# A mixture-of-experts stage regrouped: 11 units of three experts in four column groups, instead of 16 pairs in two

## The chip, the core and the metric

The program runs on one core of a Trainium2 chip, as one launch. The metric is device time in microseconds (us). The engines' names in the rows are PE (TensorE, matmul), PEld (TensorE's weight loads), DVE (VectorE), ACT (ScalarE), POOL (GpSimd) and SP (SyncE, which only issues transfers here). "L985" is line 985 of the kernel. GB and MB are decimal.

## What is computed

Two transformer blocks over 256 tokens of width 1024, in float32. The change touches the last part of the first block, a mixture of 32 experts in 4 groups of 8:

```python
def hier_moe(h, w_rg, w_re, w_e_in, w_e_out):
    t = h.reshape(-1, D)                                    # 256 tokens x 1024
    pg = softmax(t @ w_rg); gp, gi = top_k(pg, 1)           # one group of experts for each token
    le = (t @ w_re).reshape(-1, 4, 8)  # ... of the chosen group
    ew, ei = top_k(softmax(le), 2); ew = ew / sum(ew)       # two experts in it
    gates = ...                                             # [32 experts, 256 tokens], two entries for each token
    for wi, wo, ge in zip(w_e_in, w_e_out, gates):          # wi 1024x512, wo 256x1024
        a, u = split(t @ wi, 2)
        acc += ((silu(a) * u) @ wo) * ge[:, None]
```

Before it lie the token mixer of the first block, its output projection (`down` of `w_out`) and the router; behind it the second block, which begins with a norm and a feed-forward part (FFN1, 1024 to 2816 and back). Weights of the experts: 32 x (1024 x 512 + 256 x 1024) x 4 B = 100.66 MB, each read once.

## The kernel before

**Places.** Each expert gets 64 places for tokens (`CAP`). `slot` (L861 and 862) holds for each token and expert the place that the token has, from a running count made by two matmuls. `place(b)` (L827) turns it, for a block of four experts, into a 0/1 matrix `p` of 256 tokens by 256 places: DVE compares `slot` with 1 to 64. `gather` (L945) multiplies the normed tokens, split in a high and a low part (`xrh`, `xrl`, made by `gather_parts`), by that matrix, so that `xg` holds the four experts' tokens side by side, transposed. `way_back` (L959) gives the gate of each place and the transposed matrix. Tokens beyond 64 at one expert go a slow way (`beyond`, behind a branch on `mosti`, the largest load), which every engine tests for itself.

**A unit** is a pair of experts, 16 units. `in_proj` (L977) takes eight steps of k; in a step the two experts' matmuls have 64 columns of weights (`xg`, the tokens) each and 512 columns of data (the expert's w_in), and write the two halves of the partitions of one bank. `act` multiplies silu(a), u and the gate; `turn` transposes; `out_proj` (L1001) takes four steps (two halves n of the 1024 columns, two k), again two matmuls of 64 columns of weights a step; `scatter` (L1011) scales, splits in high and low parts on DVE and ACT, and adds the rows back to the tokens in four accumulators `y`. These matmuls are plain float32, and one of them stands as two instructions in the trace.

**Order.** In the loop over q (L1037), PE runs in_proj(q), way_back(q), scatter(q-1), the gather for the next block, turn(q), out_proj(q), in an order that the scheduler fixes.

**Weights.** All loads of weights are issued by SP, in order. A load waits on SP until the buffer that it fills is free, and everything behind it on SP waits too. A pool `rawp` (5 buffers of 1 MB), `hip` and `lop` (6 each of 0.5 MB) serve the whole kernel: elsewhere `raw` takes a weight panel and `hi` and `lo` its two parts. The experts use `raw` for w_in (`in_load`) and `lop`, `hip`, `gp4` in turn for w_out (`out_load`); ahead of the stage two units and a third unit's w_out are loaded, 14.7 MB, partly in `gp4` (`in_load_ahead`).

Of the kernel before, what the change touches and what calls it, by code (L numbers as in the profile page):

```python
# [9 lines left out]
F32 = mybir.dt.float32  # L10
# [12 lines left out]
CAP = 64  # L23
# [8 lines left out]
def shape_constants():  # L32
# [7 lines left out]
        np.tile(np.eye(64), (2, 2)),  # L40
        np.concatenate([k // 64 == m[:, 0:32], k // 64 == m[:, 0:32] - 2, np.tile(np.arange(1, 65)[None, :], (P, 1))], 1),
# [38 lines left out]
def body(ctx: ExitStack, tc: tile.TileContext, I, out, dbg=None):  # L80
# [14 lines left out]
    psb = ctx.enter_context(tc.tile_pool(name="psb", bufs=4, space=PSUM))  # L95

# [39 lines left out]
    def load(src, a, b):  # L136
        t = rawp.tile([P, 2048], F32, tag="raw", name="raw")
# [105 lines left out]
    V.tensor_copy(CI, v2(cst[:, 4, 0:64]))  # L243
# [174 lines left out]
    tri0 = rawp.tile([P, 2048], F32, tag="raw", name="raw")[:, 0:640]  # L418
    nc.sync.dma_start(tri0, I["cst"][:, 640:])
# [50 lines left out]
    wah = hip.tile([P, 1024], F32R, tag="hi", name="wah")[:, :512].rearrange("p (k f) -> p k f", k=KD)  # L470
# [317 lines left out]
    wi = {}  # L788

    def in_load(q, n):  # L790

        if (q, n) not in wi:
            t = rawp.tile([P, 2, 2, 512], F32, tag="raw", name="raw")
            for i in range(2):
                nc.sync.dma_start(t[:, i], I["w_expert_in"][0, 2 * q + i, 2 * n * P:(2 * n + 2) * P, :]
                                  .rearrange("(k p) f -> p k f", p=P))
            wi[q, n] = [t[:, :, k, :] for k in range(2)]

    def in_load_ahead(q, n, pool, tag):

        ts = [pool.tile([P, D], F32, tag=tag, name="wi").rearrange("p (k f) -> p k f", k=2) for _ in range(2)]
        for i in range(2):
            nc.sync.dma_start(ts[i], I["w_expert_in"][0, 2 * q + i, 2 * n * P:(2 * n + 2) * P, :]
                              .rearrange("(k p) f -> p k f", p=P))
        wi[q, n] = [[t[:, k, :] for t in ts] for k in range(2)]

    def out_load(q, pool, tag):
        halves = []
        for k in range(2):
            for i in range(2):  # L810
                t = pool.tile([P, D], F32, tag=tag, name="wo")
                nc.sync.dma_start(t, I["w_expert_out"][0, 2 * q + i, k * P:(k + 1) * P, :])
                halves.append(t)
        return halves

    for n in range(4):
        in_load(0, n)
    wo = {0: out_load(0, lop, "lo")}
    in_load(1, 0)
    wo[1] = out_load(1, hip, "hi")  # L820
    in_load_ahead(1, 1, hip, "hi")
    in_load_ahead(1, 2, lop, "lo")
    in_load_ahead(1, 3, gp4, "g4")

    places, xgs = {}, {}

    def place(b):  # L827
        p4 = t2("p4", F32R).rearrange("p (t e s) -> p t e s", t=2, e=4)
        for t in ((0, 1) if b == 0 else (slice(0, 2),)):
            n = [P, 4, 64] if b == 0 else [P, 2, 4, 64]  # L830
            V.tensor_tensor(p4[:, t], (iota64[:, None, :] if b == 0 else iota64[:, None, None, :]).to_broadcast(n),
                            slot[:, t, 4 * b:4 * b + 4, None].to_broadcast(n), op=ALU.is_equal)
        places[b] = p4.rearrange("p t e s -> p t (e s)")
        xgs[b] = []


    def tops(src, n, name, then, dt=F32):
# [22 lines left out]
    mm(pc[:, 32:64], onesr, disp[:, 0, :], start=False, stop=True, skip_group_check=True)  # L860
    slot = small(64, "slot", 1).rearrange("p (t f) -> p t f", t=2)  # L861
    placed = V.scalar_tensor_tensor(slot, pc[:, 0:64].rearrange("p (t f) -> p t f", t=2), 1.0, dispf, op0=ALU.add, op1=ALU.mult)
    place(0)

# [5 lines left out]
    gates = cp.tile([P, 2, 32], F32, name="gates")  # L870
# [8 lines left out]
    pc = bank()  # L879
    for t in range(2):  # L880
        mm(pc[:, 0:32], onesr, disp[:, t, :], start=t == 0, stop=t == 1)
    loads = small(32, "loads", 1, I32)
    V.tensor_copy(loads, pc[:, 0:32])
    most = small(1, "most")
    V.tensor_reduce(most, pc[:, 0:32], axis=AX.X, op=ALU.max)
# [88 lines left out]
    def experts(w, i):  # L974
        return w[i] if isinstance(w, list) else w[:, i, :]
# [627 lines left out]
```

## Time and profile before

| | us |
|---|---|
| median of 3 runs (1124.84 to 1125.15) | 1125.04 |
| the profiled execution | 1127.29 |
| its span, first to last instruction | 1125.4 |
| from the first in_proj matmul to the end of the last out_proj | 194.97 to 465.79 |

The span is what the rows show; the execution's own time has 1.89 us around it. The profile's page gives busy times of the engines; a busy PE is one with a matmul in flight. DMA share is the mean busy share of the 16 DMA engines, and it can read a little over 1.

### The profile page before, as it was taken

The numbers are of one execution on the slowest core, as the hardware profiler recorded it, in microseconds if no ns is written. First come the engines' busy times: TensorE is split into PE (matmuls) and PEld (weight loads), VectorE is DVE, ScalarE is ACT, GpSimd is POOL, SyncE is SP. The second block draws the span as 40 slices with busy tenths as digits, with TensorE's granted clock in tenths as the row PEclk, the third lists the DMA queues.
The fourth block names the chain that finished last, engine by engine and source line by source line (L and its number), as shares of the span: only waits on it lengthen the run. The fifth ranks groups of instructions, "written<-read, shape, count | busy, mean of one in ns | idle before, by whom it ended". The sixth has DMA issues, their size and how long they took to land.

```text
span 1125.4 us, 14826 instructions
## 1 busy us (share of the span) xinstructions
PE 1066.3 (95%) x5631; PEld 783.8 (70%) x5632; DVE 666.1 (59%) x1277; ACT 508.3 (45%) x904; POOL 5.6 (0%) x14
## 2 busy tenths in 40 slices
PE   4898998899999998799999999999999999999997
PEld 1585776444444443398888877777888888888886
DVE  3894855233322222596666469878749677666466
ACT  3634544222312211455555446584546455555453
POOL 0000000000000000000000000000000000000000
PEclk8899998999999999899999999999999999999999
DMA  9875976889999999676566634355447555656521
GB/s 377 283 280 204 365 262 260 295 311 342 355 358 380 358 326 369 198 225 199 176 208 206 202 115 156 122 172 156 145 150 261 178 176 177 209 173 220 189 92 38
DMA packets 144769, 260.64 MB, mean 232 GB/s; under 512 B 9404, under 2 KB 76200, under 8 KB 143416
## 3 DMA queue, kind: packets, MB, share of 16 engines
q1 hardware_dynamic: 144464, 259.32, 66.5%
q8 instruction: 45, 0.74, 0.3%
q10 hardware_dynamic: 232, 0.35, 0.1%
q14 instruction: 28, 0.23, 0.1%
HBM read 258.60 MB, written 1.05 MB: 231 GB/s over the span
## 4 chain that ended last, share of the span: by engine, by line
PE 73%; DVE 4%; ACT 2%; issue 1%; DMA 1%; DVEq 0%; ACTq 0%
PE mm L280 19%; PE mm L985 10%; PE mm L282 9%; PE mm L1008 5%; PE acc L302 4%; PE acc L300 4%; PE acc L304 4%; PE mm L943 3%; PE acc L1151 2%; PE acc L1150 2%; PE acc L1158 2%; PE acc L1024 2%; PE acc L1023 1%; PE acc L263 1%; PE acc L264 1%; PE acc L262 1%
## 5 line engine op out<-in xcount | busy, mean ns | idle before, releaser
L166 DVE TENSOR_TENSOR lo<-raw,hi 128x1024 fp32r<-128x1024 f32 (+1 forms) x240 | 287.2, 1205 | 161.0 <-ACT hi L165 157.1
L165 ACT CAST hi<-raw 128x1024 fp32r<-128x1024 f32 (+1 forms) x240 | 246.7, 1036 | 219.8 <-PE mm L280 94.7
L280 PE MATMUL mm<-xT,hi 128*128 128x512 f32 x832 | 209.7, 394 | 0.6 <-DVE rs L1430 0.6
L280 PEld LDWEIGHTS mm<-xT,hi 128*128 128x128 f32 x832 | 149.5, 189 | 27.5 <-DVE rs L1430 1.0
L985 PE MATMUL mm<-raw,xg 128*64 128x512 f32 x488 | 122.0, 598 | 0.0
L282 PEld LDWEIGHTS mm<-xT,lo 128*128 128x128 f32 x832 | 113.6, 190 | 8.1
L282 PE MATMUL mm<-xT,lo 128*128 128x256 f32 x832 | 116.3, 283 | 0.0
L985 PEld LDWEIGHTS mm<-raw,xg 128*64 128x64 f32 x488 | 35.1, 137 | 65.0 <-issue 61.2
L1008 PE MATMUL mm<-wo,z 128*64 128x512 f32 x256 | 58.8, 601 | 1.0 <-DVE z L999 1.0
L262 PE MATMUL acc<-hi,xT 128*128 128x512 f32 x144 | 57.7, 402 | 0.0
L263 PE MATMUL acc<-hi,xT 128*128 128x512 f32 x144 | 57.4, 398 | 0.0
L264 PE MATMUL acc<-lo,xT 128*128 128x512 f32 x144 | 57.1, 399 | 0.0
L990 ACT ACTIVATE esg<-mm 128x256 f32<-128x256 f32 x16 | 6.1, 384 | 112.6 <-PE mm L985 112.6
L956 ACT ACTIVATE xg<-mm,shT,gmT 128x256 f32<-128x256 f32 x64 | 32.3, 562 | 53.9 <-PE mm L943 52.5
L302 PE MATMUL acc<-hi,hl 128*128 128x512 f32 x176 | 55.5, 389 | 0.0
L300 PE MATMUL acc<-hi,hh 128*128 128x512 f32 x176 | 55.5, 390 | 0.0
L304 PE MATMUL acc<-lo,hh 128*128 128x512 f32 x176 | 55.5, 389 | 0.0
L1017 DVE TENSOR_TENSOR og<-mm,gtm 128x512 f32<-128x512 f32 x32 | 22.0, 688 | 40.7 <-PE mm L1008 40.7
L943 PE MATMUL mm<-p,xT 128*128 128x256 f32 x256 | 40.2, 306 | 2.1 <-DVEq L897 1.5
L991 DVE SCALAR_TENSOR_TENSOR esg<-esg,gs,mm 128x256 f32<-128x256 f32 x16 | 7.7, 480 | 57.6 <-ACT esg L990 57.6
L165 ACT CAST oh<-og 128x512 fp32r<-128x512 f32 x32 | 19.6, 618 | 47.2 <-DVE og L1017 47.1
L943 PEld LDWEIGHTS mm<-p,xT 128*128 128x128 f32 x256 | 36.4, 208 | 5.0 <-issue 3.3
(458 smaller groups left out, 1612.5 us busy)
## 6 DMA issues: line engine op xcount, KB each, us to landing
raw<-in_w_expert_in_dram SPq DMA_DIRECT2D x122, 512.0 KB
raw<-in_w_in_dram SPq DMA_DIRECT2D x32, 1024.0 KB
wo<-in_w_expert_out_dram SPq DMA_DIRECT2D x64, 512.0 KB
raw<-in_w_ada_dram SPq DMA_DIRECT2D x24, 1024.0 KB
raw<-in_ffn_w_gate_dram SPq DMA_DIRECT2D x22, 1024.0 KB
raw<-in_ffn_w_up_dram SPq DMA_DIRECT2D x22, 1024.0 KB
raw<-in_ffn_w_down_dram SPq DMA_DIRECT2D x22, 1024.0 KB
raw<-in_w_out_dram SPq DMA_DIRECT2D x8, 1024.0 KB
```

The costliest lines, as they stand in the source:

```text
L165: S.copy(hi, src)
L166: return V.tensor_tensor(lo, src, hi.bitcast(F32), op=ALU.subtract)
L262: mm(o, h_[k][:, c], hi[:, kk, z], start=k == starts, stop=False)
L263: mm(o, l_[k][:, c], hi[:, kk, z], start=False, stop=False)
L280: mm(pb, hi[:, k, :], x2[k], start=k == 0, stop=False, skip_group_check=True)
L282: mm(pb[:, 0:256], lo[:, k, :], x2[k][:, 0:256], start=False, stop=k == nk - 1, skip_group_check=True)
L300: mm(pa[t][n], hh[k][:, c], hi[:, 0, n * 512:(n + 1) * 512], start=k == seq[0], stop=False)
L302: mm(pa[t][n], hl[k][:, c], hi[:, 0, n * 512:(n + 1) * 512], start=False, stop=False)
L304: mm(pa[t][n], hh[k][:, c], lo[:, 0, n * 512:(n + 1) * 512], start=False, stop=k == seq[-1])
L943: mm(pb[:, kk * 256:(kk + 1) * 256], (xrh, xrl)[i][:, t, k * P:(k + 1) * P], places[b][:, t, :], start=i == 0 and t == 0 and kk == 0, stop ...
L985: mm(st_["hp"][64 * i:64 * i + 64, :], xgs[q // 2][k // 4][:, k % 4, 64 * e:64 * e + 64], experts(wi[q, k // 2][k % 2], i), start=k == 0, ...
L1008: mm(oo[n][r, :], st_["z"][:, k, r], wo[q][2 * k + i][:, c], start=k == 0, stop=k == 1, skip_group_check=True)
```

## The change

The 32 experts form 11 units of three (the last of two). A unit has four column groups of 32 places: group 0 is shared, groups 1 to 3 belong to the three experts. Whichever expert of the unit has more than 32 tokens (the first such) also owns the shared group, as its places 33 to 64. In the last unit, groups 0 and 1 belong to its first expert, groups 2 and 3 to its second.

```diff
-CAP = 64
+NU = 11
+CAP = 32
...
-    rawp = ctx.enter_context(tc.tile_pool(name="rawp", bufs=5))
-    hip = ctx.enter_context(tc.tile_pool(name="hip", bufs=6))
-    lop = ctx.enter_context(tc.tile_pool(name="lop", bufs=6))
+    def weight_pools(**pools):
+        panels.close()
+        wp_.clear()
+        for name, bufs in pools.items():
+            wp_[name] = panels.enter_context(tc.tile_pool(name=name, bufs=bufs, reuse_waits="tile"))
+    weight_pools(rawp=5, hip=6, lop=6)
...
+    weight_pools(mwp=14)
+    def unit_load(src, e):
+        t = wp_["mwp"].tile([P, 3, 512], F32, tag="mw", name="mw")
+        nc.sync.dma_start(t[:, :len(e)], src.rearrange("e p f -> p e f"))
+        return t
+    def unit_loads(u):
+        e = experts[u]
+        a, b = e[0], e[-1] + 1
+        if u < NU and (u, 0) not in wi:
+            for k in range(KD):
+                wi[u, k] = unit_load(I["w_expert_in"][0, a:b, k * P:(k + 1) * P, :], e)
+            for n in range(2):
+                for k in range(2):
+                    wo[u, k, n] = unit_load(I["w_expert_out"][0, a:b, k * P:(k + 1) * P, n * 512:(n + 1) * 512], e)
+    for u in range(2):
+        unit_loads(u)
...
-    slot = small(64, "slot", 1).rearrange("p (t f) -> p t f", t=2)
+    slot = small(66, "slot", 1).rearrange("p (t f) -> p t f", t=2)
...
+    V.tensor_copy(many[:, 0:32], pc[:, 64:96])
+    V.tensor_scalar(own, many.rearrange("p (u i) -> p u i", i=3), CAP + 0.5, None, op0=ALU.is_gt)
...
+    V.tensor_reduce(slot4[:, :, 0:NU - 1, 0], owned[:, :, 0:NU - 1], axis=AX.X, op=ALU.add)
...
     place(0)
...
-        with tc.If(over > CAP):
+        with tc.If(over > 0):
...
+    def tiles_of(q, w):
+        if q == NU - 1:
+            return [w[:, 0], w[:, 0], w[:, 1], w[:, 1]]
+        i = nc.s_assert_within((owner >> (2 * q)) & 3, 0, 2, skip_runtime_bounds_check_because=
+                               "at most one of a unit's two bits is set: its second or its third expert is the owner")
+        return [w[:, bass.ds(i, 1)]] + [w[:, i] for i in range(3)]
...
-            for i in range(2):
-                e = (2 * q + i) % 4
-                mm(st_["hp"][64 * i:64 * i + 64, :], xgs[q // 2][k // 4][:, k % 4, 64 * e:64 * e + 64],
-                   experts(wi[q, k // 2][k % 2], i), start=k == 0, stop=k == KD - 1, skip_group_check=True)
+            for i, w in enumerate(tiles_of(q, wi[q, k])):
+                c = 128 * (q % 2) + 32 * i
+                mm(st_["hp"][32 * i:32 * i + 32, :], xgs[q // 2][k // 4][:, k % 4, c:c + 32], w,
+                   start=k == 0, stop=k == KD - 1, skip_group_check=True)
...
+    owner = nc.values_load(owners[0:1, 0:1], engines=[mybir.EngineType.PE], min_val=0, max_val=4 ** 11 - 1)
...
-    scattered = scatter(prev, NQ - 1)
+    scattered = scatter(prev, NU - 1)
+    weight_pools(rawp=5, hip=6, lop=6)
```

out_proj changes as in_proj does: four matmuls of 32 columns a step. While the stage runs, the memory of the three pools is one ring `mwp` of 14 tiles; a tile holds one k (or one k and half n of w_out) of all experts of a unit, 3 x 128 x 512 floats or 0.786 MB (0.524 MB in the last unit), so a unit takes 12 tiles, 8 for in_proj and 4 for out_proj, and there are 132. A new tile waits only for the tiles whose memory it takes. The owners of all units are packed in one integer that PE reads into a register, from which the address of the shared group's weights is worked out. The diff also does the same regrouping for the gates (`gate4`, `gsplit`), and small things that follow: a smaller table of constants, `vrow` in another pool, single buffers in `tops`.

On SP, at the start of the stage, before (the places `raw`, `wo`, `wi` are buffers for expert weights, `mosti` the number on which the branch to the slow way hangs):

```order
L795 DMA raw<-in_w_expert_in_dram 128x2x512 x8
L812 DMA wo<-in_w_expert_out_dram 128x1024 x3
L795 DMA raw<-in_w_expert_in_dram 128x2x512 x2
L812 DMA wo<-in_w_expert_out_dram 128x1024 x5
L803 DMA wi<-in_w_expert_in_dram 128x2x512 x6
L812 DMA wo<-in_w_expert_out_dram 128x1024 x4
L896 TENSOR_LOAD mosti
L896 ISA x2
L795 DMA raw<-in_w_expert_in_dram 128x2x512 x10
L897 COMPARE_AND_BRANCH
```

and in the changed kernel (`mw` is a tile of the ring; the eighteen rows of the slow way behind the branch are not shown):

```order
L805 DMA mw<-in_w_expert_in_dram 128x3x512 x8
L805 DMA mw<-in_w_expert_out_dram 128x3x512 x4
L805 DMA mw<-in_w_expert_in_dram 128x3x512 x8
L805 DMA mw<-in_w_expert_out_dram 128x3x512 x4
L942 TENSOR_LOAD mosti
L943 COMPARE_AND_BRANCH
```

The loads of two whole units now stand ahead of SP's branch, 24 tiles for a ring of 14, and 12 each for the units that follow it.

On DVE, between the count of places and the first matrix of places, before (`teo` marks a token's two experts, `xT` is the low part of the tokens):

```order
L850 TENSOR_SCALAR teo<-tew 128x64
L862 SCALAR_TENSOR_TENSOR slot<-mm,teo 128x64
L883 CAST loads<-mm 128x32
L831 TENSOR_TENSOR p_1590<-cst,slot 128x256 x2
L869 TENSOR_REDUCE gp<-e_1593 128x2
```

and in the changed kernel the last twelve of the rows from there to the matrix (`slot_1615` is `slot4`, the places by unit and column group):

```order
L878 MEMSET own 128x2
L795 SCALAR_TENSOR_TENSOR xT_99<-xres,rmsz,xT_99 128x1024
L882 TENSOR_TENSOR owned<-slot,own 128x66
L892 SCALAR_TENSOR_TENSOR which<-own 128x11
L912 TENSOR_TENSOR ws<-ws,gp 128x2
L884 TENSOR_REDUCE slot_1615<-owned 128x2x10
L893 TENSOR_TENSOR which<-which,cst 128x11
L913 RECIPROCAL ws<-ws 128x2
L887 TENSOR_SCALAR slot_1615<-slot_1615 128x22
L895 TENSOR_REDUCE ownsum<-which 128x1
L914 TENSOR_TENSOR gate_1638<-gate_1638,ws 128x2x32
L832 TENSOR_TENSOR p_1623<-cst,slot_1615 128x256 x2
```

Where one instruction (`loads`) stood between `slot` and `p`, there are now 23: 22 on at most 128 x 66 elements and, among them, the first of the two 128 x 1024 instructions that make `xT`.

On PE, from the first gather to the first in_proj, before:

```order
L881 MATMUL mm<-teo,cstr 128x32 x2
L943 MATMUL mm<-p_1590,xT_99 128x256 x32
L985 MATMUL mm<-raw,xg 64x512 x16
L964 MATMUL mm<-gsplit,p_1590 128x4 x2
L985 MATMUL mm<-raw,xg 64x512
```

and in the changed kernel:

```order
L991 MATMUL mm<-p_1623,xT_99 128x256
L1081 TENSOR_LOAD owners
L1081 ISA x2
L991 MATMUL mm<-p_1623,xT_99 128x256 x31
L1040 REGISTER_ALU
L1040 ISA
L1040 MATMUL mm<-mw,xg 32x512 x4
```

PE reads `owners` behind the first matmul of the gather, and from then on each step of four matmuls has one or two register instructions and one more ahead of it.

## Rows read from the trace of the kernel before

**Rows 1.** The page, busy us of each engine, share of the span, instructions.
```profile
PE 1066.3 (95%) x5631; PEld 783.8 (70%) x5632; DVE 666.1 (59%) x1277; ACT 508.3 (45%) x904; POOL 5.6 (0%) x14
```

**Rows 2.** Windows: length; busy us of PE, PEld, DVE, ACT, POOL; clock; DMA share, GB/s.
```profile
195.00:467.00 272.00, 261.35 (x1220) 117.07 (x1220) 74.12 (x152) 59.26 (x113) 0.00 (x0) 0.99 0.94 343
320.00:360.00 40.00, 39.58 (x197) 18.52 (x196) 12.25 (x24) 10.59 (x20) 0.00 (x0) 1.00 1.04 396
380.00:410.00 30.00, 28.37 (x138) 13.63 (x138) 7.67 (x17) 7.11 (x14) 0.00 (x0) 1.00 1.03 376
210.00:220.00 10.00, 8.08 (x38) 4.95 (x38) 2.24 (x6) 2.45 (x6) 0.00 (x0) 0.83 0.72 264
470.00:480.00 10.00, 5.96 (x25) 5.34 (x26) 8.86 (x26) 9.05 (x20) 0.00 (x0) 0.51 0.01 2
```

**Rows 3.** The chain that ended last, one unit of it: start us, us, what.
```profile
309.64 3.58 PE mm L985 x16
...
314.55 3.58 PE mm L985 x16
...
321.61 3.58 PE mm L1008 x16
325.19 3.43 PE mm L985 x16
```

**Rows 4.** Timeline of PE early on, start us, us: four column groups of 32.
```profile
29.60 2.78 PE L353 MATMUL acc<-raw,sT 128*32 128x512 f32 x24
32.31 1.06 PE L359 MATMUL acc<-b,cst 12*32 12x512 f32 x8
```

**Rows 5.** Timeline of SP: issues of expert weights, start us, us from first to last.
```profile
136.82 18.18 SPq L795 DMA_DIRECT2D raw<-in_w_expert_in_dram  x8
...
162.78 16.03 SPq L812 DMA_DIRECT2D wo<-in_w_expert_out_dram  x5
178.90 3.83 SPq L803 DMA_DIRECT2D wi<-in_w_expert_in_dram  x6
```

**Rows 6.** Waits of SP: who for whom, us in total, times, longest us.
```profile
SPq L795 <- PE mm L985: 110.5, 33, 7.9
...
SPq L897 <- SPq L897: 4.0, 4, 1.4
```

**Rows 7.** Timeline from the count of places to the first in_proj.
```profile
187.62 0.23 DVE L862 SCALAR_TENSOR_TENSOR slot<-mm,teo 128x64 f32<-128x64 f32 x1 [0.76 <-PE mm L860]
...
188.16 0.75 DVE L831 TENSOR_TENSOR p<-cst,slot 128x256 fp32r<-128x256 f32 x2
...
188.63 6.30 PE L943 MATMUL mm<-p,xT 128*128 128x256 f32 x32 [0.62 <-DVE p L831]
188.82 0.15 DVE L869 TENSOR_REDUCE gp<-e 128x2 f32<-128x8 f32 x1
...
189.28 0.14 DVE L887 CAST mosti<-most 128x1 int32<-128x1 f32 x1
189.34 1.28 DVE L784 SCALAR_TENSOR_TENSOR xT<-xres,rmsz,xT 128x1024 fp32r<-128x1024 f32 x1
...
194.97 7.09 PE L985 MATMUL mm<-raw,xg 128*64 128x512 f32 x32
```

**Rows 8.** Timeline of PE from the second in_proj's end to the first out_proj.
```profile
210.68 0.39 PE L964 MATMUL mm<-gsplit,p 128*128 128x4 f32 x2
...
213.42 1.46 PE L943 MATMUL mm<-p,xT 128*128 128x256 f32 x8 [1.50 <-DVEq L897]
...
216.94 3.95 PE L1008 MATMUL mm<-wo,z 128*64 128x512 f32 x16
```

**Rows 9.** Timeline of the last out_proj and FFN1's first splits (`hi`).
```profile
462.14 3.65 PE L1008 MATMUL mm<-wo,z 128*64 128x512 f32 x16 [0.52 <-DVE z L999]
...
473.86 1.03 ACT L165 CAST hi<-raw 128x1024 fp32r<-128x1024 f32 x1
...
479.96 2.00 ACT L165 CAST hi<-raw 128x1024 fp32r<-128x1024 f32 x2
```

More of the change, by code (lines that the diff above doesn't have):

```diff
@@ L136, in load @@
     def load(src, a, b):
-        t = rawp.tile([P, 2048], F32, tag="raw", name="raw")
+        t = wp_["rawp"].tile([P, 2048], F32, tag="raw", name="raw")
         v = t[:, : a * b].rearrange("p (a b) -> p a b", a=a)
@@ L807, in out_load @@
[L807 to L821, printed above, removed]
@@ new lines, in body @@
+    V.tensor_copy(slot4[:, :, :, 1:4], slotu)
+    V.tensor_reduce(slot4[:, :, 0:NU - 1, 0], owned[:, :, 0:NU - 1], axis=AX.X, op=ALU.add)
+    V.tensor_copy(slot4[:, :, NU - 1, 0], slot[:, :, 30])
+    V.tensor_copy(slot4[:, :, NU - 1, 3], slot[:, :, 31])
+    V.tensor_scalar(slot4[:, :, :, 0], slot4[:, :, :, 0], -float(CAP), None, op0=ALU.add)
+    placed = V.tensor_scalar(slot4[:, :, NU - 1, 3], slot4[:, :, NU - 1, 3], -float(CAP), None, op0=ALU.add)
+    place(0)
+    which = small(11, "which", 1)
@@ L865, in body @@
+    V.scalar_tensor_tensor(which, own[:, :, 2], 2.0, own[:, :, 1], op0=ALU.mult, op1=ALU.add)
+    V.tensor_tensor(which, which, pow4, op=ALU.mult)
+    ownsum = small(1, "ownsum")
+    V.tensor_reduce(ownsum, which, axis=AX.X, op=ALU.add)
+    owners = small(1, "owners", 1, I32)
+    V.tensor_copy(owners, ownsum)
     e4 = small(8, "e4").rearrange("p (t n) -> p t n", t=2)
@@ L878, in body @@
     V.tensor_tensor(gates, gates, ws[:, :, None].to_broadcast([P, 2, 32]), op=ALU.mult)
-    pc = bank()
-    for t in range(2):
-        mm(pc[:, 0:32], onesr, disp[:, t, :], start=t == 0, stop=t == 1)
+    limit = small(33, "limit", 1)
+    V.tensor_scalar(limit, own.rearrange("p u i -> p (u i)"), float(CAP), float(CAP), op0=ALU.mult, op1=ALU.add)
+    V.tensor_tensor(many, many, limit, op=ALU.subtract)
+    V.tensor_scalar(many, many, 0.0, None, op0=ALU.max)
     loads = small(32, "loads", 1, I32)
-    V.tensor_copy(loads, pc[:, 0:32])
+    V.tensor_copy(loads, many[:, 0:32])
     most = small(1, "most")
-    V.tensor_reduce(most, pc[:, 0:32], axis=AX.X, op=ALU.max)
+    V.tensor_reduce(most, many[:, 0:32], axis=AX.X, op=ALU.max)
     mosti = small(1, "mosti", dt=I32)
@@ L1038, in body @@
     prev = None
-    for q in range(NQ):
+    for q in range(NU):
         cur = {}
-        for n in range(4):
-            in_load(q, n)
-        if q not in wo:
-            wo[q] = out_load(q, *((lop, "lo"), (hip, "hi"), (gp4, "g4"))[q % 3])
+        unit_loads(q)
         if q == 2:
             fng = row_bcast(t4("fng"), I["final_norm_g"], D)
-        if q % 2 == 0 and q // 2 + 1 < NE // 4:
+        if q % 2 == 0 and q // 2 + 1 < NB:
             place(q // 2 + 1)
@@ L1310, in body @@
     rope_T(iqT, pq, 8, 32)
-    wn = rawp.tile([P, KD, 256], F32, tag="raw", name="raw")
+    wn = wp_["rawp"].tile([P, KD, 256], F32, tag="raw", name="raw")
     for i, c0 in enumerate((512, 1152)):
```

139 lines of the change are left out of this document (78 added, 61 removed).

## The prediction

> **What bounds the kernel now.** I read the page first: PE has a matmul in flight for 95% of the span [rows 1]. A busy PE is not a PE at its peak, so the next view is the windows over the stage that changes. From the first in_proj (194.97) to the end of the last out_proj, 462.14 + 3.65 = 465.79 [rows 9], PE is busy 261.35 of 272 us, at a clock of 0.99 of its 2.4 GHz [rows 2]. The chain of waits agrees: inside a unit it stays on PE, and goes from in_proj at 309.64 to the next in_proj at 325.19, so 15.55 us a unit [rows 3]. Sixteen of these are 249 us of the 271. So PE bounds this stage. But the same windows show a second resource right behind it: the DMA engines are busy 0.94 of the stage and bring 343 GB/s, and where nothing holds them, from 320 to 360, it is 396 GB/s at a share of 1.04 [rows 2]. SP waits 110.5 us in all for in_proj matmuls to free a buffer [rows 6]: this is what keeps the stream below 396. A change that only shortens PE's work has 396/343, so about 13%, before the stream is the bound. I put E at the end of the last out_proj; everything behind it is the same work.
>
> **PE's part.** A step of two matmuls with 64 columns costs 3.58 us / 4 = 0.90 us (sixteen instructions are eight matmuls, so four steps) [rows 3]. The trace has a row for four groups of 32 columns as well: three such steps go from 29.60 to 32.31, 0.90 us each [rows 4]. So a step keeps its price, and 16 x 12 = 192 steps become 11 x 12 = 132: 60 x 0.90 = 54 us of PE's work go. Gather, scatter and turn of a unit keep their sizes (128 places), so five whole units go, 5 x 15.55 = 78 us. If PE stayed the bound, that would be the gain.
>
> **The stream's part.** The bytes stay: 100.66 MB. Rate: where the DMA share is over 1, the windows have 396 GB/s (320 to 360) and 376 (380 to 410) [rows 2]; these are the ends, with the stage's mean of 343, which has SP's holds in it, as the far one. I take 390, nearer to the upper end, since in the changed kernel PE is the one that waits and most of the 14 tiles are always on order. A ring tile is 0.786 MB, 2.02 us, so a unit of twelve needs 24.2 us against 15.55 of PE. The stream becomes the bound, and the sum goes by it.
>
> Start S of the first in_proj, 194.97 before [rows 7]. Between `slot` and `p` 21 more small DVE instructions stand, and the 1.28 us one for `xT`. A small one costs between 0.115 us (four steps from 188.82 to 189.28, independent ones) and 0.27 us (two from 187.62 to 188.16) [rows 7]; so 3.7 to 7.0 us, and I take 0.165 each, nearer to the independent rows because three chains are interleaved: 4.8 us. PE's read of `owners` in the middle of the gather is not in this trace; the nearest row is the branch on a loaded number, behind which PE was idle 1.50 us [rows 8]; between 0 and 1.5, I take 1.5, since the gather's rest stands behind it on PE. PE idles longer ahead of the gather, which then runs longer at the lower clock level: the 6.30 us of its 32 instructions [rows 7] hold such a part already, I add 0.7. S = 194.97 + 4.8 + 1.5 + 0.7 = 202.0.
>
> What is loaded by S: 14 tiles, 11.0 MB (before 14.7). SP's loads began at 136.82, and five issues that began at 162.78 took until 178.90, held by buffers of the output projection [rows 5]; the ring lies on the same memory, so up to eight tiles start then and take 16 us: landed by 196, ahead of S. The delay of S is thus not hidden: the ring is full and the stream stands still until PE frees a tile.
>
> The first two units: eight tiles come free by the first in_proj, the stream runs from S + 0.9 to S + 0.9 + 8 x 2.02 = S + 17.0. Tile 22 needs the memory of the first w_out tile, which the first out_proj frees. The second in_proj waits for tile 19, landed at about S + 14.8, and ends at S + 15.7; from there to the first out_proj it was 210.68 to 216.94, 6.3 us [rows 8]; one step more and a microsecond from issue to data make S + 24.0. So the stream idles from S + 17.0 to S + 24.0, 7 us. SP's branch now stands behind tile 23; its waits there were 1.4 us at the longest [rows 6], and the 4 us of tiles 22 and 23 hide it. Without that cover it would cost those 1.4 us.
>
> From there it runs through: 98 tiles of 0.786, 12 of 0.524 and the 0.524 of `fng`, 83.9 MB, at 390 GB/s 215.1 us, to S + 239.1 = 441.1. One us to landing and the last step of 0.90: 443.0. In a unit PE holds back a tile for at most the 15.55 - 12 x 0.90 = 4.8 us of other work, 2.4 tiles of 14, so the ring does not run dry behind it; the register instructions ahead of each step hide in the 8.6 us a unit that PE waits. I add 1 us because the last steps may run at the lower clock. E = 444.0, 21.8 us earlier.
>
> Behind E: FFN1's panels can only be loaded when ring tiles come free, before they lay ready. `gain`, then gate and up, 2.6 MB, need 6.7 us behind the last expert tile; the first split comes 473.86 - 465.79 = 8.1 us after E, the next pair's 14.2 us after it [rows 9], for which 4.7 MB or 12.1 us are needed. Cover is there but thin: 0 to 4 us, I take 2. Overwritten constants, `vrow`, single buffers in `tops`: nothing, they lie beside loads or add no instruction to PE.
>
> **Sum.** The profiled execution's 1127.29 becomes 1127.29 - 21.8 + 2 = 1107.5. It lies 2.25 us above the median of the runs; from the median the same gain gives 1105.2, so 1105.
>
> **Rivals.** (a) *The stream doesn't hold its rate.* Tiles now gather rows of three experts that lie far apart, and half rows of w_out. They start at S + 24.0 = 226.0, and with the 1.9 us behind them and the 1 and 2 us of the two small costs the gain is gone when 83.9 MB take 465.8 - 226.0 - 4.9 = 234.9 us, at 357 GB/s. At the stage's mean of 343 they take 244.6 us, 9.7 longer than that: 1135. Against it: the rows of a full stream have 376 and 396. The Trainium skill (DMA: Bandwidth & Descriptors, Specifications) gives a limit of about 358 GB/s of HBM for one core; by that rule the stream takes 234.4 us and the result would be about 1124.5, no change. The row of 396 GB/s over 40 us speaks against the rule here.
> (b) *PE becomes the bound again, and slower.* There are 465.8 - 202 = 263.8 us for eleven units, 24.0 each. PE would exceed that if each step's register instructions cost it over (24.0 - 15.55) / 12 = 0.70 us, or if over 54% of its work ran at the lower clock level. For it: PE will wait in every step, and where it was busy 5.96 of 10 us the granted clock was 0.51, with 8.08 of 10 it was 0.83 [rows 2]; its new share would be 15.55 of 24.2, 64%. Against it: its gaps are near 1.1 us, and a PE at half speed would be busy all the time, which everywhere in this stage goes with a clock near 1. Wholly at half speed, 11 x 31.1 = 342 us, it would end at 544: about 1203; at three quarters 11 x 27.2, E = 501, about 1160.
> (c) *The stream has no gap at all:* 89.65 MB right from S at 396, 226.4 us, E = 431, and no cost at FFN1: about 1090. Against it stands the ring's order at the first out_proj.
> (d) *It doesn't do what it says:* tokens over the limit send every engine through the slow way. Counted from the reference on its inputs, the fullest expert has 47 tokens (with 7 and 25 in its unit), two others 34, each alone over 32 in its unit; so nothing overflows.
>
> **How the numbers follow.** My forecast, 1094 to 1114, which covers a stream of 376 to 400 GB/s, S from 199 to 206 and FFN1 from 0 to 4, gets 0.62. A gain left, but smaller (stream between 358 and 376, or gaps in every unit), 1114 to 1122.8: 0.12. Within 0.2%, which is about what a measurement of this kernel can tell from no change: 0.06, (a) near 357 GB/s. Slower: 0.13, of it 0.05 (a) and 0.08 (b). Below 1094, (c): 0.06. (d) 0.01. The range leaves out all that is slower or the same and a little of (c), and goes from 1090 to 1122. Faster 0.80, same 0.06, slower 0.14.
>
> **What would show it.** In the changed kernel's windows over the expert stage the DMA share should stand at 1.0 and above from some 25 us after the first in_proj, at about 390 GB/s, and PE's idle time in front of in_proj and out_proj should name the DMA of `mw`. A step of four should take 0.90 us. The first in_proj should start near 202, and the stream should pause once, before the first out_proj. The last out_proj should end near 444. I am wrong if the stream reads below 360 with PE waiting (a), or if PE is busy throughout with a DMA share below 1 (b), or if FFN1's first split waits for `raw`.

## The result, and the profile after

The changed kernel takes 1106.8 us (median of 4 runs, 1106.39 to 1107.57), the kernel before 1125.1 beside it: a ratio of 0.983 (95% interval 0.9815 to 0.985). The prediction was 1105, within 1090 to 1122. The profiled execution has a span of 1105.2 us, 20.2 less than before. The last out_proj ends at 446.16 + 1.06 = 447.22 (before 465.79, [rows 9]), 18.6 earlier. What stands behind it takes 658.0 us instead of 659.6, which is the other 1.6.

The page of the changed kernel, engines, as in [rows 1]:

```profile
PE 999.8 (90%) x5785; PEld 734.5 (66%) x5786; DVE 646.2 (58%) x1258; ACT 491.6 (44%) x873; POOL 5.6 (1%) x14
```

Windows of the changed kernel, columns as in [rows 2]: ahead of the stage, its start, the first out_proj, and the steady stretch.

```profile
140.00:180.00 40.00, 40.00 (x218) 30.93 (x219) 22.27 (x56) 18.55 (x31) 0.00 (x0) 1.00 0.11 37
180.00:190.00 10.00, 6.22 (x36) 4.45 (x34) 5.86 (x34) 5.76 (x10) 0.00 (x0) 0.93 0.98 359
220.00:230.00 10.00, 5.86 (x38) 4.17 (x30) 1.56 (x5) 1.41 (x3) 0.00 (x0) 0.83 1.03 357
230.00:430.00 200.00, 160.55 (x1119) 60.77 (x1117) 44.87 (x86) 35.45 (x68) 0.00 (x0) 0.97 1.05 387
```

For 200 us on end the DMA share is 1.05 and the rate 387 GB/s, against 0.94 and 343 over the stage before. PE is busy 160.55 of these 200 us. So the bound has gone from PE to the stream. The other windows hold a surprise: from 140 to 180 almost nothing is loaded, and around the first out_proj the rate dips to 357, but there is no pause.

The timeline of PE shows a step as it is now, and the end of the stage:

```profile
211.36 1.07 PE L1040 MATMUL mm<-mw,xg 128*32 x8 [0.97 <-DMA mw<-in_w_expert_in_dram]
213.40 1.06 PE L1040 MATMUL mm<-mw,xg 128*32 x8 [0.97 <-DMA mw<-in_w_expert_in_dram]
...
436.73 3.64 PE L1040 MATMUL mm<-mw,xg 128*32 128x512 f32 x32
...
442.34 2.78 PE L1062 MATMUL mm<-mw,z 128*32 128x512 f32 x24 [0.52 <-DVE z L1054]
445.73 0.50 PE L1076 MATMUL acc<-oh,back 128*128 128x512 f32 x1 [0.60 <-ACT oh L177]
446.16 1.06 PE L1062 MATMUL mm<-mw,z 128*32 128x512 f32 x8
```

Steps stand 2.04 us apart, which is the time of one tile, and PE waits 0.97 of it for the DMA. At the end, in the last unit, only the first step of in_proj still waits for the DMA (0.37 us, at 429.14).

### The profile page after: what moved, and what is told of

The parts are those of the page before. It is cut to its first block, busy times and chain, and to the rows that moved or that the text cites. A ratio compares the mean times of both kernels' runs of the same rounds, so it can differ in the third digit from the quotient of the medians.

```text
span 1105.2 us, 15399 instructions
## 1 busy us (share of the span) xinstructions
PE 999.8 (90%) x5785; PEld 734.5 (66%) x5786; DVE 646.2 (58%) x1258; ACT 491.6 (44%) x873; POOL 5.6 (1%) x14
## 3 DMA queue, kind: packets, MB, share of 16 engines
HBM read 258.54 MB, written 1.05 MB: 235 GB/s over the span
## 4 chain that ended last, share of the span: by engine, by line
PE 60%; DMA 11%; DVE 5%; ACT 2%; issue 1%; DVEq 0%; SPq 0%; ACTq 0%
PE mm L291 19%; PE mm L293 9%; DMA mw<-in_w_expert_in_dram 8%; PE acc L313 4%; PE acc L315 4%; PE acc L311 4%; PE mm L1040 2%; DMA mw<-in_w_expert_out_dram 2%; PE acc L1202 2%; PE mm L1062 2%; PE acc L1201 2%; PE acc L1209 2%; PE acc L274 1%; PE acc L275 1%; PE acc L273 1%; PE mm L991 1%
## 5 line engine op out<-in xcount | busy, mean ns | idle before, releaser
L178 DVE TENSOR_TENSOR lo<-raw,hi 128x1024 fp32r<-128x1024 f32 (+1 forms) x240 | 287.3, 1205 | 160.2 <-ACT hi L177 156.4
L1040 PE MATMUL mm<-mw,xg 128*32 (+1 forms) x704 | 89.2, 604 | 25.5 <-DMA mw<-in_w_expert_in_dram 24.5
L293 PE MATMUL mm<-xT,lo 128*128 128x256 f32 x832 | 112.1, 277 | 0.0
L1040 PEld LDWEIGHTS mm<-mw,xg 128*32 128x32 f32 x704 | 16.9, 108 | 78.8 <-DMA mw<-in_w_expert_in_dram 47.8
L1005 ACT ACTIVATE xg<-mm,shT,gmT 128x256 f32<-128x256 f32 (+1 forms) x48 | 23.3, 546 | 89.2 <-PE mm L991 89.0
L1062 PE MATMUL mm<-mw,z 128*32 128x512 f32 (+1 forms) x352 | 46.2, 642 | 5.3 <-DMA mw<-in_w_expert_out_dram 4.6
L1070 DVE TENSOR_TENSOR og<-mm,gtm 128x512 f32<-128x512 f32 x22 | 15.2, 691 | 45.4 <-PE mm L1062 45.4
L991 PE MATMUL mm<-p,xT 128*128 128x256 f32 (+1 forms) x192 | 34.6, 326 | 7.5 <-DVE p L832 3.9
L1201 PE MATMUL acc<-hi,xT 128*128 128x256 f32 (+1 forms) x120 | 36.9, 332 | 2.4 <-ACT xT L177 2.3
L311 PEld LDWEIGHTS acc<-hi,hh 128*128 128x128 f32 x176 | 32.9, 188 | 7.4
L315 PEld LDWEIGHTS acc<-lo,hh 128*128 128x128 f32 x176 | 33.1, 188 | 7.1
```

The lines of the kernel that those rows point to most:

```text
L178: return V.tensor_tensor(lo, src, hi.bitcast(F32), op=ALU.subtract)
L293: mm(pb[:, 0:256], lo[:, k, :], x2[k][:, 0:256], start=False, stop=k == nk - 1, skip_group_check=True)
L311: mm(pa[t][n], hh[k][:, c], hi[:, 0, n * 512:(n + 1) * 512], start=k == seq[0], stop=False)
L315: mm(pa[t][n], hh[k][:, c], lo[:, 0, n * 512:(n + 1) * 512], start=False, stop=k == seq[-1])
L1040: mm(st_["hp"][32 * i:32 * i + 32, :], xgs[q // 2][k // 4][:, k % 4, c:c + 32], w, start=k == 0, stop=k == KD - 1, skip_group_check=True)
L1062: mm(oo[n][r, :], st_["z"][:, k, r], w, start=k == 0, stop=k == 1, skip_group_check=True)
```

## The experiments

"E" is the end of the last out_proj in the profiled execution (start plus length of its row), "behind" is the span minus E. The ratio is to the kernel before on the same chip. E is from one execution each, and where the first in_proj starts differs between these although the work up to there is the same: 200.30 in the changed kernel, 196.53 in e3, 196.65 in e6. So differences of E below 4 us are not read as an effect of an edit.

| | us, median | ratio (95%) | E | behind |
|---|---|---|---|---|
| before | 1125.1 | 1 | 465.8 | 659.6 |
| changed kernel | 1106.8 | 0.983 (0.981 to 0.985) | 447.2 | 658.0 |
| e1, two thirds of the bytes | 1055.2 | 0.938 (0.935 to 0.940) | 394.0 | 659.0 |
| e2, pairs on a ring | 1146.6 | 1.018 (1.016 to 1.021) | 488.4 | 659.6 |
| e3, no register | 1106.3 | 0.983 (0.981 to 0.985) | 444.0 | 658.6 |
| e4, pieces of 6 KB | 1090.3 | 0.968 (0.965 to 0.970) | 428.9 | 659.5 |
| e5, pairs on a ring, PE's order held | 1113.2 | 0.988 (0.986 to 0.989) | 452.3 | 659.5 |
| e6, ring filled early | 1108.5 | 0.983 (0.981 to 0.986) | 448.0 | 658.0 |
| e7, and the first out_proj early | 1101.4 | 0.977 (0.975 to 0.980) | 442.1 | 658.1 |
| e8, pieces of 4 KB | 1100.5 | 0.978 (0.975 to 0.980) | 431.7 | 665.3 |
| e9, pools moved by 64 bytes | 1115.1 | 0.991 (0.989 to 0.992) | 447.8 | 666.4 |
| e10, pools moved by 96 bytes | 1106.6 | 0.982 (0.981 to 0.984) | 436.1 | 668.4 |
| e11, what helped, together | 1092.5 | 0.971 (0.969 to 0.973) | 428.5 | 660.7 |
| e12, and the ring moved by 96 bytes | 1084.4 | 0.963 (0.961 to 0.965) | 421.4 | 660.2 |

**e1: is it the bytes?** On the changed kernel:

```diff
-        nc.sync.dma_start(t[:, :len(e)], src.rearrange("e p f -> p e f"))
+        m = min(len(e), 2)
+        nc.sync.dma_start(t[:, :m], src[0:m].rearrange("e p f -> p e f"))
...
-        return [w[:, bass.ds(i, 1)]] + [w[:, i] for i in range(3)]
+        return [w[:, bass.ds(i & 1, 1)]] + [w[:, i] for i in (0, 1, 1)]
```

> The third expert of each unit is not loaded (its column group multiplies the second's weights); the matmuls, their order and the ring stay. Theory (the stream of weights sets the stage): 69 MB instead of 100.7 MB at 387 GB/s would be on chip 81 us earlier, and PE becomes the bound with 15.55 us a unit; 200.3 + 11 x 15.55 + some 20 us of start and end puts the end of the last out_proj near 390 instead of 447, and the whole near 1050. Rival (PE sets the stage by its steps of four, with their register instructions): the steps are the same, so the end stays near 447 and the whole near 1107.

Measured: 1055.2 us, E 394.0. The matmuls are the same and 52 us are gone, so the changed kernel is bound by its bytes. Here PE comes near to being the bound again, and the DMA share falls below 1 (windows of e1):

```profile
320.00:360.00 40.00, 37.86 (x270) 13.61 (x270) 10.17 (x21) 7.51 (x15) 0.00 (x0) 1.00 0.95 329
```

**e2 and e5: the ring without the regrouping.** e2 is the kernel before with its pairs of 64, but all its expert weights go through one ring:

```diff
+    weight_pools(mwp=21)
...
+    def unit_load(src):
+        t = wp_["mwp"].tile([P, 2, 512], F32, tag="mw", name="mw")
+        nc.sync.dma_start(t, src.rearrange("e p f -> p e f"))
...
-            in_load(q, n)
...
+        unit_loads(q)
```

> The kernel before with 16 pairs of 64 places, but its expert weights go through one ring of 21 tiles of 128 x 2 x 512 that lies on the memory of the three pools, as in the changed kernel. Theory A of the prediction (before, PE is the bound with 15.55 us a unit, so only the regrouping brings the gain): the last out_proj ends near 465, the whole near 1125. Rival B (the stream bound both: a pair takes 6.29 MB, 16.3 us at 387 GB/s, more than PE's 15.55, and the old pools held it back to 343 GB/s): with the ring alone the stream runs without a gap from 180, the end comes near 447 to 452, and the whole near 1107 to 1112.

Neither theory had 1146.6 us. The timeline of PE in e2 shows why: the scheduler, which fixes PE's order, has put single steps of in_proj between the matmuls of scatter.

```profile
314.93 3.65 PE L1001 MATMUL mm<-mw,z 128*64 128x512 f32 x16
318.51 0.50 PE L1016 MATMUL acc<-oh,back 128*128 128x512 f32 x1
319.03 0.50 PE L1017 MATMUL acc<-ol,back 128*128 128x512 f32 x1
319.46 1.08 PE L978 MATMUL mm<-mw,xg 128*64 128x512 f32 x4
320.47 0.51 PE L1016 MATMUL acc<-oh,back 128*128 128x512 f32 x1
...
333.75 3.65 PE L1001 MATMUL mm<-mw,z 128*64 128x512 f32 x16
```

From one out_proj to the next it is 18.82 us. A step that stands alone takes 1.01 us to the next matmul instead of 0.90, scatter's matmuls take longer too (462 and 460 ns in the mean, 422 and 399 in e5), and PE waits 11.0 us in all for DVE's part of `act`, in e5 not at all. e5 is e2 with PE's order held from the third unit on:

```diff
+        if q == 2:
+            as_written.enter_context(tc.manual_schedule(engines={mybir.EngineType.PE}))
```

> As e2_ring_pairs, pairs of 64 on the ring, but PE's order from the third unit on is held to the order in which the loop is written. In e2 the scheduler had laid single steps of in_proj between the matmuls of scatter, and a unit took 18.8 us (314.93 to 333.75) instead of 15.55. Theory B (the stream bounds pairs on a ring too): 16.3 us a unit, DMA at 387 GB/s throughout, last out_proj near 447 to 452, the whole 1105 to 1113. Theory A (PE bounds the pairs, as the prediction said): 15.55 us a unit and some 22 us of start, last out_proj near 466, the whole near 1125, DMA near 370 GB/s. Were the order not the cause of e2's loss, it would stay at 1146.

Measured: 1113.2 us, E 452.3, as theory B has it. A window of e5:

```profile
240.00:320.00 80.00, 77.90 (x391) 37.03 (x390) 25.21 (x49) 19.92 (x37) 0.00 (x0) 1.00 1.05 386
```

and two out_proj that follow each other in its timeline of PE:

```profile
339.76 3.65 PE L1001 MATMUL mm<-mw,z 128*64 128x512 f32 x16
...
355.69 3.65 PE L1001 MATMUL mm<-mw,z 128*64 128x512 f32 x16
```

The stream runs at 386 GB/s with the old pairs too, while PE is busy 77.90 of 80 us. A unit of 15.93 us and 6.29 MB (16.3 us at 386 GB/s) are nearly the same, so the two bounds lay side by side. Of the 18.6 us by which E came earlier, 13.5 are to be had by the ring with PE's order held; the regrouping adds 5.1 to that (the ratios, 0.988 and 0.983, give the same). With the order as the scheduler leaves it, the regrouping is worth 41 us on the ring (488.4 to 447.2). The changed kernel has such lone steps too, but there PE has the time. Why the scheduler chose that order for e2 stays open. Neither the regrouping on the old pools was tried nor the order held on them, so how much of the 13.5 is the ring's and how much the order's was not shown.

**e3: do the register instructions cost PE?**

```diff
...
-        return [w[:, bass.ds(i, 1)]] + [w[:, i] for i in range(3)]
+        return [w[:, i] for i in (0, 0, 1, 2)]
...
-    owner = nc.values_load(owners[0:1, 0:1], engines=[mybir.EngineType.PE], min_val=0, max_val=4 ** 11 - 1)
```

> The shared group always takes the first expert's weights, so PE reads no owners and works out no address: no register instruction ahead of a step. Theory (PE waits for the stream in every step and hides them): within 1 us of the changed kernel, 1106 to 1108. Rival (the register instructions cost PE what rival (b) of the prediction says): each of 132 steps gains 0.1 us or more, so 13 us or more, under 1095.

Measured: 1106.3 us, the same. (Its profiled execution, the one in the table, was its fastest; there E comes 3.2 us earlier, but the first in_proj already 3.8.) In the changed kernel the register instructions are short, and lie in front of matmuls that wait for a tile (those of line 1040; ns, shortest, median, longest):

```profile
L1040 PEldq ALU_OP  x152: 32/36/45, 197.4 to 417.5; - x152
L1040 PEldq FUSED_REGOPS  x80: 46/46/46, 197.5 to 417.6; - x80
```

**e4 and e8: the length of a piece.** In the changed kernel every piece that lies in one row in DRAM and in one row of a tile is 2 KB. e4 takes 6 KB, of other rows:

```diff
-        nc.sync.dma_start(t[:, :len(e)], src.rearrange("e p f -> p e f"))
+        m = len(e)
+        nc.sync.dma_start(t[:, :m], src.rearrange("(p r) f -> p r f", r=m))
...
```

> A tile takes 384 rows of 2 KB that lie one behind the other in DRAM (three a partition, 6 KB in one piece) instead of three times 128 rows, 2 KB in one piece; same bytes, other rows of the same experts, so other products. Theory R (the rate of the stream hangs on the length of a piece; before, a third of the bytes came in pieces of 4 KB and the full stretch read 396, now all come in 2 KB and read 387): the stretch reads 400 to 420 GB/s, the stage ends 8 to 20 us earlier, the whole 1087 to 1099. Rival (387 is the ceiling of the engines or the memory whatever the rows): 387 GB/s and 1105 to 1108.

e8 takes 4 KB everywhere, and the tokens in the order of rows that goes with it:

```diff
-    weight_pools(mwp=14)
+    weight_pools(mwp=7)
...
+                rows = I["w_expert_in"][0, a:b, 2 * j * P:2 * (j + 1) * P, :]
+                wi[u, 2 * j], wi[u, 2 * j + 1] = unit_load(rows.rearrange("e (p r) f -> p e (r f)", r=2), e)
...
-                mm(pb[:, kk * 256:kk * 256 + w], (xrh, xrl)[i][:, t, k * P:(k + 1) * P], places[b][:, t, :],
+                mm(pb[:, kk * 256:kk * 256 + w], (xrh, xrl)[i][:, t, 2 * k2 * P + kk:2 * (k2 + 1) * P:2], places[b][:, t, :],
```

> The changed kernel with a ring of seven tiles of double size: partition p takes two neighbouring rows of w_in, 4 KB in one piece, and whole rows of w_out, also 4 KB; the gather takes every second column of the tokens, so that the sums are the same. Theory R (the rate hangs on the length of a piece; e4 read 417 GB/s with 6 KB, and the mixture of 2 and 4 KB before, 396, gives some 415 for 4 KB): from 180 on 260 x 387/415 = 242 us, stream's end near 422 to 424, last out_proj near 430, the whole 1088 to 1092. Rival (e4's gain came from which rows lie side by side, not from the length): 387 GB/s and 1105 or, with the coarser ring, more.

A window of e4:

```profile
320.00:360.00 40.00, 32.26 (x230) 13.05 (x230) 9.44 (x18) 7.54 (x14) 0.00 (x0) 1.00 1.02 417
```

and the same window of e8:

```profile
320.00:360.00 40.00, 32.87 (x238) 13.40 (x233) 10.55 (x19) 7.80 (x13) 0.00 (x0) 0.97 1.03 409
```

Theory R holds: 387, 409 and 417 GB/s for 2, 4 and 6 KB. e4 gives 1090.3 us. e8's E of 431.7 is near the expected 430, but its 1100.5 us are not the expected 1088 to 1092, since the work behind E had grown from 658 to 665 us. That work reads no expert weights, and nothing in it had been edited; e9 looks for the cause.

**e6 and e7: the start of the stream.** In the changed kernel the ring's second tile lies on memory of `lo`, which the last matmuls of the output projection free at 179. e6 fills the places on `raw` first:

```diff
-    weight_pools(mwp=14)
+    weight_pools(mwp=1)
+    ring = [5, 4, 3, 2, 1, 0, 10, 9, 13, 8, 12, 7, 11, 6]
...
+        t = ring_tile(ring[(len(wi) + len(wo)) % 14])
...
```

> The changed kernel with the same ring of 14, filled in another order of places: first the six on the memory of the panels (raw), which comes free by 160, then those on hi and lo, in the order in which these come free. Theory (the prediction's start: then the ring is full before the first in_proj and the stream stands twice, before it and before the first out_proj): six tiles instead of one by 162, 5 x 2.03 us ahead; it stands some 5 us before 201 and some 5 us near 220; the stream ends 0 to 3 us earlier, the whole 1103 to 1107. Rival (the late start is simply lost time): the end comes 10 us earlier, near 1097.

e7 adds to it, in the second unit:

```diff
+            if q == 1:
+                turn(prev)
+                out_proj(prev, 0)
             in_proj(cur, q, 0)
...
+            with tc.manual_schedule(engines={mybir.EngineType.PE}):
+                scatter(prev, 0)
             beyond()
...
-                turn(prev)
...
-                out_proj(prev, 0)
...
```

> e6_early, and the first turn, out_proj and scatter moved ahead of the second in_proj and of the branch, so that the tiles of the first w_out come free near 213 instead of 230. Theory: only the wait before the first in_proj stays; 118 tiles from 201.2 on, 106 x 2.03 + 12 x 1.36 + 1.4 = 233 us, end of the stream 434, last out_proj 441, the whole near 1100. Rival (the place of the first out_proj doesn't matter): as e6.

Windows of e6:

```profile
190.00:200.00 10.00, 9.35 (x64) 6.79 (x67) 2.82 (x13) 5.00 (x10) 0.00 (x0) 0.74 0.22 68
220.00:230.00 10.00, 8.97 (x54) 4.58 (x54) 3.70 (x6) 3.11 (x6) 0.00 (x0) 0.87 0.54 183
```

e7 came as its theory has it, 1101.4 us. e6 took 1108.5, a little above the expected 1103 to 1107 and far from its rival's 1097. e6 has the two stops that the prediction had drawn: the ring is full ahead of the first in_proj, the stream stands there (68 GB/s) and once more before the first out_proj (183). Its first in_proj and the end of the stage, in the timeline and the windows of e6:

```profile
196.65 7.07 PE L1047 MATMUL mm<-mw,xg 128*32 x64
```
```profile
416.00:428.00 12.00, 9.97 (x47) 3.46 (x43) 2.29 (x4) 1.81 (x4) 0.00 (x0) 0.57 1.05 386
440.00:444.00 4.00, 2.46 (x23) 0.62 (x19) 0.91 (x2) 0.38 (x1) 0.00 (x0) 1.00 0.09 37
```

and the last of these windows in the changed kernel:

```profile
440.00:444.00 4.00, 2.46 (x22) 0.75 (x22) 0.91 (x2) 0.39 (x1) 0.00 (x0) 1.00 0.77 292
```

In this execution the stream of e6 ends some 3 us earlier, near 441, but the first in_proj stands 3.65 us earlier already. Counted from there the stream ends no sooner (244 us in both), so what the early start brought is given back at the stops. E itself, 448.0, is not the stream's: from 416 to 428 the granted clock was 0.57, and PE then came last, some 7 us behind the stream. With the first out_proj early (e7) only one stop is left, and E comes 5.1 us earlier than in the changed kernel (the medians 5.4).

**e9 and e10: where the pools lie.** Nothing but an unused buffer, of 64 bytes in e9 and 96 in e10:

```diff
+    small(16, "pad", 1)
```

> The changed kernel, and nothing but an unused small buffer of 64 bytes a partition, which moves raw, hi and lo (the panels of weights and their parts) from byte 138912 to 138976, as in e8, where a group of 16 matmuls of the second feed-forward part came every 2.807 us instead of 2.774 and the work behind the last out_proj took 665 us instead of 658. Theory P (the place of hi and lo sets that): 2.807 here too, 104 groups and the like of them in the other panels, 6 to 7 us, the whole 1112 to 1114. Rival (e8's later work was slower for another reason): 2.774 and 1106 to 1108.

> The same with 96 bytes, which puts raw, hi and lo on multiples of 128 bytes (139008). So far: remainder 32 in the changed kernel 2.774 us a group, 64 in the kernel before, e2 and e5 2.793, 96 in e8 2.807. Theory P: the series goes on to some 2.75 to 2.76 at remainder 0, 2 to 5 us less behind the experts, the whole 1102 to 1105. Rival: the remainder has nothing to do with it, 2.774 and 1106 to 1108.

Groups of instructions on PE, one line of the feed-forward parts (busy us in all, mean ns of one | idle before). In the changed kernel:

```profile
L293 PE MATMUL mm<-xT,lo 128*128 128x256 f32 x832 | 112.1, 277 | 0.0
```

in e9:

```profile
L295 PE MATMUL mm<-xT,lo 128*128 128x256 f32 x832 | 115.8, 281 | 0.0
```

and in e10:

```profile
L295 PE MATMUL mm<-xT,lo 128*128 128x256 f32 x832 | 117.0, 282 | 0.0
```

e9 settles e8's loss: 64 bytes, and the work behind E takes 666.4 us, the whole 1115.1. The lines of PE behind E that got slower are those that read `hi` or `lo`. In e10 the panels' matmuls are slower still, 668.4 us behind E, so the series did not go on as theory P had it. But the whole stays at 1106.6, since E came 11.1 us earlier. The windows of e10 say why:

```profile
240.00:320.00 80.00, 66.95 (x492) 26.22 (x484) 18.39 (x38) 13.50 (x27) 0.00 (x0) 0.98 1.05 407
```

The stream, still in pieces of 2 KB, reads 407 GB/s instead of 387. The place of the ring sets its rate, and e12 moves the ring alone.

**e11 and e12: a faster version.** e11 is e8 with e7's start, PE's order held as in e5, the last unit's turn and out_proj ahead of the scatter before it, and the pools at 138912 as in the changed kernel. e12 adds one buffer of 96 bytes in front of the ring, and only while the experts run:

```diff
-    weight_pools(mwp=1)
+    weight_pools(gap=1, mwp=1)
+    wp_["gap"].tile([P, 24], F32, tag="gap", name="gap")
```

> What the runs so far point to, together: pieces of 4 KB (e8), the ring filled from the panels' memory first and the first out_proj early (e7), hi and lo where the changed kernel has them (138912), PE's order held as written from the third unit on, and in the last unit turn and out_proj ahead of the scatter of the unit before, so that less is left to do behind the last tile. Theory (start + bytes / rate + tail): seven tiles by 195, the stream stands until 201, then 90.2 MB at 408 GB/s = 221 us, end 422, last out_proj 3 to 5 us behind it, near 426, and 658 us from there: span 1084, the whole 1084 to 1088. Rival (behind the gain of the rate PE is the bound: e8 had already PE busy 82% of the stretch 320 to 360): not under 1095.

> e11_best, and only the ring moved by 96 bytes, to 139008, a multiple of 128; raw, hi and lo stay at 138912 behind and ahead of the experts. In e10 the same 96 bytes for the ring and the panels together raised the stream of the experts from 387 to 407 GB/s (last out_proj 11 us earlier) and lengthened the work behind it from 658 to 668.4 us. Theory D (the ring's place sets the rate, the place of hi and lo the panels' matmuls, one without the other): the stream reads 420 to 430 GB/s instead of 409, the last out_proj comes near 420 to 422 instead of 428.5, the work behind it stays at 660.7, the whole 1082 to 1086. Rival 1 (with pieces of 4 KB the place no longer matters): 409 GB/s, 1091 to 1094. Rival 2 (it was not the place of hi and lo that lengthened the work behind): 670 us behind the last out_proj, and no gain in all.

A window of e11:

```profile
320.00:360.00 40.00, 28.25 (x202) 10.61 (x202) 9.31 (x18) 6.05 (x10) 0.00 (x0) 0.96 1.03 409
```

the same of e12:

```profile
320.00:360.00 40.00, 31.48 (x220) 14.46 (x224) 8.69 (x17) 7.59 (x14) 0.00 (x0) 0.96 1.03 421
```

and the last out_proj in e12's timeline of PE:

```profile
417.58 3.86 PE L1084 MATMUL mm<-mw,z 128*32 128x512 f32 x32 [0.52 <-DVE z L1076]
```

e11 takes 1092.5 us, above the expected 1084 to 1088: E is 428.5 where 426 was expected, and the work behind it 660.7 where 658 was, since the scatter of two units now stands there. e12 takes 1084.4 and is within its forecast on all three counts (421 GB/s, E 421.4, 660.2 behind). By the ratios 0.963 and 0.983 it is some 2% faster than the changed kernel, and 3.7% faster than the kernel before.

## Why the prediction was right, and where it was not

**The bound.** That PE's work is cut and the stream takes over is what happened, and the rate decides: taken 390, measured 387. On 83.9 MB that is 1.7 us. That PE alone bounded the kernel before was too simple a reading. [rows 3] give 15.55 us of PE a unit, but the stage took 16.9 (270.8 / 16), and a unit's bytes need 16.3 at 387 GB/s. SP's holds in [rows 6] were thus not only the reason for 343 GB/s: with them gone and PE's order held, most of the gain was there without the regrouping (e5). The forecast held all the same, because its sum goes by bytes over rate, whatever PE does.

**PE's step.** Taken 0.90 us for four groups of 32; four steps take 3.64, so 0.91. The register instructions hide, as it said (e3).

**S.** Predicted 202.0, measured 200.3. The parts were less alike (timeline of the changed kernel from the count of places to the first in_proj):

```profile
189.41 0.23 DVE L870 SCALAR_TENSOR_TENSOR slot<-mm,teo 128x64 f32<-128x64 f32 x1 [1.05 <-PE mm L863]
...
192.71 0.75 DVE L832 TENSOR_TENSOR p<-cst,slot 128x256 fp32r<-128x256 f32 x2
...
194.47 5.89 PE L991 MATMUL mm<-p,xT 128*128 128x256 f32 x31 [0.65 <-DVE gate L935]
...
200.30 1.06 PE L1040 MATMUL mm<-mw,xg 128*32 x8
```

From `slot` to `p` it is 3.30 us instead of 0.54 in [rows 7], 2.8 more where 4.8 were taken: less the 1.28 of `xT`, the 22 small instructions take 0.09 us each, below the lower end of 0.115. PE's stop for `owners` was 0.65 (taken 1.5), and the gather itself took 6.44 us, 0.1 more (taken 0.7). `slot` came 1.8 later than in [rows 7], but that is not the change: in e3, with the same code up to there, it came 3.3 us earlier:

```profile
186.10 0.23 DVE L870 SCALAR_TENSOR_TENSOR slot<-mm,teo 128x64 f32<-128x64 f32 x1 [0.93 <-PE mm L863]
...
196.53 4.06 PE L1038 MATMUL mm<-mw,xg 128*32 128x512 f32 x34
```

So the change itself delays S by some 3.5 us where 7.0 were taken; that 200.3 lies so near to 202.0 is luck of the execution.

**The preload and the pause.** This step was wrong. "Landed by 196, ahead of S", "the ring is full and the stream stands still" did not come about. SP's timeline has the issue of the first eight tiles, and its waits (us in total, times, longest) what held the second:

```profile
159.85 24.95 SPq L805 DMA_DIRECT2D mw<-in_w_expert_in_dram  x8
```
```profile
SPq L805 <- PE acc L315: 19.7, 3, 19.2
```

and PE's last matmul but two of this line, which reads `lo`:

```profile
179.01 0.39 PE L315 MATMUL acc<-lo,cah 128*128 128x512 f32 x1
```

The first tile is issued at 159.85, the second only at 179.4. The prediction had taken from the old kernel's issues in [rows 5] that much of the memory comes free early, but had not looked at which tile lies on which memory. By 200 some 8 MB were in (0.8 and, by the rates up to there, 3.6 and 3.9), not 11.0. In return the stream never stood ahead of S, and did not pause for 7 us at the first out_proj. The errors nearly cancel, and that was luck: the 2.7 MB that were missing take 7.0 us at 387 GB/s, as long as the pause that was not there. The last tile was to land at 442.1; unit 9's last tile is there at 427.7 (PE waits for it until then), and twelve of 1.36 us later it is 444.0. Of these 1.9 us 1.7 are the rate's. e6 shows the other half: with the full ring and both stops the stream ends no sooner after the first in_proj, so the preload was worth nothing by itself. A small slip lies in the pause too: by the prediction's own terms tile 19 lands at S + 0.9 + 6 x 2.02 + 1, so S + 14.0, not S + 14.8.

**The tail.** From the landing of the last tile the prediction took 0.9 us for a step and 1 for the clock; it was 447.2 - 444.0 = 3.2. The rows at the end of the stage show PE, not the stream, in the last place: half of in_proj until 440.4, act and turn until 442.3, then out_proj, with a matmul of scatter ahead of its last step that waits for `oh`. The last unit's tiles have two thirds of the size and come every 1.36 us, so there PE falls behind. This term was too small by 1.3 us. The 1 us for the clock was not needed here (1.00 from 416 to 447; in e6 it was 0.57 from 416 to 428).

**FFN1.** Taken 2 us, measured none: the first split is at 455.04 in the changed kernel, 7.8 us behind E, where it was 8.1. And not counted at all: behind E the work itself is 1.6 us shorter. The pools' remainder by 128 bytes has changed from 64 to 32, and e9 shows that such a change can move this work by 8 us. The two largest lines of panel matmuls take 326.0 us before and 323.9 in the changed kernel. But e4 has 323.9 there too and 659.5 behind E, so that the 1.6 come from this was not shown.

The sum for the span was 21.8 - 2 = 19.8, measured 20.2. **The rivals:** (a) fell: the stream reads 387 GB/s, above the 357 at which the gain would have been gone. The Trainium skill's limit of about 358 GB/s of HBM for one core (DMA: Bandwidth & Descriptors, Specifications) did not bind with one core at work; e12 read 421. (b) fell with e3, and the granted clock was 0.97 from 230 to 430 although PE was busy only 160.55 of these 200 us. (c) had the right picture, a stream almost without a gap, but E came 16 us later than it said, with the late start and at 387 GB/s. (d) did not occur.

## What to carry to other kernels

Where one engine is busy 95% of a stage, work out the second bound per unit too, from bytes and the best window's rate; if the two lie within a few per cent, find what holds the second back before cutting the first. A ring is worth what its first tiles' memory allows, so look up which old buffer each of them lies on. And when the stream is the bound, try longer pieces and another place for its buffers: here each was worth over 5% of the rate at 2 KB. Choose that place for the ring alone, since the place of other buffers that matmuls read has a price of its own.

## What the runs showed of the hardware that was not expected

**A price for each piece.** As an estimate, a piece's time on one of 16 DMA engines is its bytes x 16 / rate: 84.7 ns for 2 KB (387 GB/s) and 80.5 with the ring at byte 139008 (407), 160.2 for 4 KB (409) and 156.0 at 139008 (420, the mean over e12's windows). So the place costs 4.2 ns a piece at both lengths, and 2 KB more cost 75.5 ns, which leaves 5.0 ns a piece. From these three numbers 6 KB at 138912 should take 5.0 + 3 x 75.5 + 4.2 = 235.7 ns, 417 GB/s, as e4 read. Byte 138976 (e9) brought nothing. The Trainium skill (DMA: Bandwidth & Descriptors, How a descriptor splits into AXI transactions) says that a descriptor is cut into transactions of 256 bytes, and that the first transaction of one that starts off a multiple of 256 bytes starts at the boundary below. The Trainium skill tells it of bytes that are fetched; here it is the place written that was moved. The runs agree so far: 139008 is a multiple of 256, 138912 and 138976 are not. A multiple of 64 is not enough: the ring of e5, with remainder 64 by 128, read 386 GB/s. Whether 128 would do no run shows, nor what the side of DRAM does.

**The place of matmul operands.** The same work behind E took between 658 and 668 us, by the byte at which raw, hi and lo begin: remainder by 128 of 32, 658 to 659.5; 64, 659.5; 96, 665 to 666; 0, 668. e12, which moved only the ring, kept 660.2, so it is the place of these pools. Between 32 and 64 the totals do not tell a difference. Which of the three, and by what rule, stays open; a neighbour's 64 bytes can cost more than an edit brings.

**The scheduler's order.** With the same matmuls of the pairs on the ring, the whole took 33 us less with the order held (e2 and e5).
